# The first feed-forward of a decoder layer: from chunks of 352, 344 and 344 tokens to chunks of 128, 456 and 456

## The chip, the cores and the metric

The kernel runs on one core of a Trainium2 chip. A core has a matrix engine (TensorE, PE in the profile), a vector engine (VectorE, DVE), a scalar engine (ScalarE, ACT), a general engine (GpSimd, POOL), and a queue engine (SyncE, SP) that here issues most of the DMA transfers. Each engine works through its own instructions in order and waits on semaphores of the others. The metric is the device time of one execution, in microseconds (us); lower is better.

## The reference, cut to what matters

One layer over T = 16 + 1024 = 1040 tokens with D = 1024 and D_FF = 2816. The change lies in the first line of the sum:

```python
h = h + 0.5 * swiglu(rms_norm(h, ffn1_norm), ffn1_w_in, ffn1_w_out)      # "FFN1"
u = rms_norm(h, mix_norm) @ w_in
o = concat([hgrn2(...u...), stick_breaking(...u...)])
h = h + o @ w_out
h = h + 0.5 * swiglu(rms_norm(h, ffn2_norm), ffn2_w_in, ffn2_w_out)      # "FFN2"

def swiglu(h, w_in, w_out):
    g, u = split(h @ w_in, 2)              # w_in 1024 x 5632
    return (silu(g) * u) @ w_out           # w_out 2816 x 1024
```

All of it is in float32. The kernel splits each operand x of a product into a rounded part xh and a remainder xl = x - xh, and multiplies three times: wh xh, wl xh, wh xl.

## The kernel before, in words

Activations lie transposed: features on the 128 partitions, tokens along the free axis. A matmul loads a 128x128 block of weights (the stationary operand) and streams the tokens of a chunk past it. FFN1 cuts the 1040 tokens into THIRDS (line 29): 352, 344 and 344. Chunk 0 is computed plainly. Chunks 1 and 2 are the two columns of a 2x2 block matrix, multiplied by the seven-product (Strassen-Winograd) scheme: blocks B11, B21 (chunk 2), B22 and B12 (chunk 1), combinations T1 to T4 of them, and combinations of weight blocks made by POOL (`made`, L290 to L292). Seven products of each 2x2 block stand in for eight.

*Input product* (`fast_in`, L262). Weight columns come in pairs of 128; a `quad` (L339) computes such a pair for gate or up half: products B11, T2, B21, T3, T1, T4, B22 of twelve matmuls each, into PSUM banks qa, qb, qc, and beside them the four plain products of chunk 0 (`alone`, L325, bank qd), 84 + 48 matmuls a quad, 22 quads. Each weight block is split in `operand` (L275): wh on ACT (L277), wl on DVE (L279), three buffers; raw blocks of 256 KB come in through SP with eight buffers. The gate goes through Silu on ACT, the up half is multiplied on DVE (L418 to L428), and POOL makes the combinations T1 to T4 of the activations for the output product (`combined`, L434 to L450) and stores them to DRAM. The first three weight pairs ("openers") run their six plain quads ahead, while rows of chunks 2 and 1 are still loaded, normalised (`norm_rows`, L640), transposed on PE (`turned`, L623, tile xps), evicted and combined (`first_block` L669, `first_combined` L685: differences on DVE, halved by `halve` L218, ACT L222 and DVE L223). Between quads, `turn_x` (L711) transposes the residual rows and stores them as xD.

*Output product* (`fast_out`, L489). First `plain_round` (L544): chunk 0 over all 22 blocks of w_out, eight PSUM banks, 528 matmuls of 352 columns at L554; it is issued after a point inside the last quads (`issue_after(self.last_p1)`), so that its loads come during them. Then seven steps A12, A11, S1, S2, S4, S3, A22 (L569 on), each over q = 0 to 10, twelve matmuls a q (L588), 924 of 344 columns. A q's weights (`left`, L523) and activations (`right`, L509) are split by `halved` (L514: L516 ACT, L518 DVE, four buffers); the ring of raw blocks has five. `load_h` brings the residual hT (eight loads). The RMS norm of the next block (`norm_steps`, L1430) runs beside the steps, one chunk at a time, and ends in the early k and v projection (`project_early`, L1501).

The order on PE is that of the program text (`manual_schedule`). The order on DVE, ACT, POOL and SP is set by a list scheduler when the program is built, from the text's order, priorities and its own estimates; on the chip each engine then follows that list. A tile waits for what last used its buffer, and a new pool waits, tile by tile, for what used the same memory before.

## Time and profile before

| | us |
|---|---|
| runs, median (lowest to highest) | 2103.28 (2100.52 to 2104.81) |
| profiled execution, span | 2101.1 |
| PE busy | 2028.4 (97%) |
| DVE busy | 1392.3 (66%) |
| ACT busy | 901.4 (43%) |
| POOL busy | 647.1 (31%) |
| FFN1: first product / last input product / last output product ends at | 15.2 / 502.1 / 741.4 |

The profile gives each engine's busy time, windows of it, single instructions with their line and tiles (an instruction's `out<-in`), and a chain of waits followed back from the last instruction. "idle before <- releaser" is the time an engine stood still ahead of an instruction and what ended it. The kernel's times and the span are of different executions.

### The profile page before, as it was taken

Reading aid. Unit: us, or ns where it says so; the run is one execution under the profiler, and the core shown is the slowest. Engines: PE = TensorE matmul, PEld = TensorE weight load, DVE = VectorE, ACT = ScalarE, POOL = GpSimd, SP = SyncE. Lnnn points to the kernel's source line nnn. Section 1 sums busy time; section 2 is a strip of 40 time slices with the busy share of each in tenths; the row PEclk is TensorE's granted clock in tenths of the full one; section 3 lists DMA queues with packets and bytes.
Section 4 is the critical chain, followed back from the end, with each engine's and each line's share of the span. In section 5 each row is a group of like instructions: output and inputs, shape, how many; then the busy total and the mean of one; then the engine's idle time right before and its main releaser. Section 6 shows DMA issues by size and latency. Waiting matters only on the chain.

```text
span 2101.1 us, 32170 instructions
## 1 busy us (share of the span) xinstructions
PE 2028.4 (97%) x11520; PEld 1830.6 (87%) x11520; DVE 1392.3 (66%) x2140; ACT 901.4 (43%) x1860; POOL 647.1 (31%) x710
## 2 busy tenths in 40 slices
PE   7999999999999999999999998998999999999998
PEld 6999999999999999988897887886788888878887
DVE  6875544555489942258878776659776676677674
ACT  8543333333465634456666514235233233234443
POOL 2475545452000002243334200012554464430000
PEclk9999999999999999999999999999999999999999
DMA  7643333325867635435454162234533332358364
GB/s 198 190 146 121 110 111 104 98 80 197 254 207 223 220 116 166 156 108 138 119 142 131 51 242 87 81 118 135 162 103 100 111 105 91 107 193 267 111 200 136
DMA packets 272566, 301.12 MB, mean 143 GB/s; under 512 B 24694, under 2 KB 199158, under 8 KB 272406
## 3 DMA queue, kind: packets, MB, share of 16 engines
q1 hardware_dynamic: 254710, 248.62, 39.1%
q0 software_dynamic: 16656, 50.44, 6.5%
q8 instruction: 91, 1.49, 0.3%
q14 instruction: 69, 0.57, 0.1%
q10 hardware_dynamic: 1040, 0.00, 0.0%
HBM read 216.42 MB, written 82.57 MB: 142 GB/s over the span
## 4 chain that ended last, share of the span: by engine, by line
PE 83%; DVE 7%; ACT 2%; issue 1%; DMA 0%; POOL 0%; SPq 0%; DVEq 0%; ACTq 0%; POOLq 0%
PE o L588 16%; PE qb L320 13%; PE qc L320 9%; PE qa L320 8%; PE qd L320 6%; PE proj L163 5%; PE proj L164 5%; PE proj L165 5%; PE o L554 4%; PE flip L1070 2%; PE lvl L839 2%; PE wo L164 1%; PE wo L163 1%; PE wo L165 1%; DVE keep L1216 1%
## 5 line engine op out<-in xcount | busy, mean ns | idle before, releaser
L320 PE MATMUL qb<-T,wh 128*128 128x344 f32 (+1 forms) x1056 | 311.6, 358 | 9.7 <-DVE u L362 5.8
L279 DVE TENSOR_TENSOR wl<-s,wh 128x512 fp32r<-128x512 f32 x176 | 202.5, 1151 | 112.6 <-ACT wh L277 109.9
L588 PE MATMUL o<-tl,wh 128*128 128x344 f32 (+1 forms) x616 | 219.1, 357 | 5.1 <-DVE tl L518 5.1
L320 PEld LDWEIGHTS qb<-T,wh 128*128 128x128 f32 x1056 | 193.0, 189 | 35.3 <-ACT wh L277 7.5
L588 PE MATMUL o<-th,wl 128*128 128x344 f32 (+1 forms) x616 | 218.8, 357 | 2.5 <-DVE wl L518 2.5
L588 PE MATMUL o<-th,wh 128*128 128x344 f32 (+1 forms) x616 | 218.6, 357 | 0.0
L320 PE MATMUL qa<-B,wh 128*128 128x344 f32 (+1 forms) x704 | 209.3, 361 | 0.0
L277 ACT CAST wh<-s 128x512 fp32r<-128x512 f32 x176 | 109.4, 622 | 224.5 <-PE qb L320 154.6
L163 PE MATMUL proj<-xh,wh 128*128 128x344 f32 (+2 forms) x576 | 204.9, 356 | 0.0
L164 PE MATMUL proj<-xh,wl 128*128 128x344 f32 (+2 forms) x576 | 199.5, 346 | 1.1 <-DVE wl L150 1.1
L165 PE MATMUL proj<-xl,wh 128*128 128x344 f32 (+2 forms) x576 | 198.7, 345 | 0.0
L279 DVE TENSOR_TENSOR wl<-raw,wh 128x512 fp32r<-128x512 f32 x172 | 153.4, 896 | 68.1 <-ACT wh L277 61.9
L277 ACT CAST wh<-raw 128x512 fp32r<-128x512 f32 x172 | 105.8, 620 | 194.0 <-PE qc L320 96.0
L320 PE MATMUL qb<-T,wl 128*128 128x344 f32 (+1 forms) x528 | 188.3, 357 | 0.0
L320 PE MATMUL qd<-X,wh 128*128 128x352 f32 x704 | 180.5, 324 | 1.3 <-DVE X L665 1.3
L516 ACT CAST th<-act 128x512 fp32r<-128x512 f32 (+2 forms) x176 | 95.2, 542 | 182.3 <-PE o L588 126.6
L292 POOL TENSOR_TENSOR s<-raw 128x512 f32<-128x512 f32 x88 | 125.0, 1421 | 94.4 <-DVE wl L279 70.1
L518 DVE TENSOR_TENSOR tl<-act,th 128x512 fp32r<-128x512 f32 (+2 forms) x176 | 105.7, 604 | 68.6 <-ACT th L516 68.6
L320 PEld LDWEIGHTS qa<-B,wh 128*128 128x128 f32 x704 | 128.6, 189 | 16.1
L588 PEld LDWEIGHTS o<-tl,wh 128*128 128x128 f32 x616 | 116.6, 190 | 19.3 <-DVE tl L518 6.9
L1216 DVE TENSOR_TENSOR_SCAN keep<-keep 128x144 f32<-128x144 f32 (+6 forms) x112 | 128.5, 1150 | 6.5 <-ACT keep L1212 4.4
L588 PEld LDWEIGHTS o<-th,wl 128*128 128x128 f32 x616 | 116.4, 189 | 15.9 <-DVE wl L518 3.8
(329 smaller groups left out, 4886.7 us busy)
## 6 DMA issues: line engine op xcount, KB each, us to landing
raw<-in_ffn_w_in_dram SPq DMA_DIRECT2D x208, 256.0 KB, 3.1
raw<-in_ffn_w_out_dram SPq DMA_DIRECT2D x176, 256.0 KB, 3.9
raw<-in_w_in_dram SPq DMA_DIRECT2D x28, 512.0 KB, 4.3
ks<-kD SPq DMA_DIRECT2D x32, 260.0 KB, 5.2
ak<-in_ffn_w_out_dram SPq DMA_DIRECT2D x22, 256.0 KB, 4.2
v<-vD SPq DMA_DIRECT2D x8, 576.0 KB, 5.0
hT<-xD SPq DMA_DIRECT2D x8, 520.0 KB, 7.5
xD<-xts POOLq DMA_DIRECT2D x16, 256.0 KB, 2.9
```

The lines of the kernel that those rows point to most:

```text
L163: nc.tensor.matmul(ps, wh[:, s], xs, start=k == 0, stop=False)
L164: nc.tensor.matmul(ps, wl[:, s], xs, start=False, stop=False)
L165: nc.tensor.matmul(ps, wh[:, s], xl[:, k, c0 : c0 + n], start=False, stop=k == nk - 1)
L277: nc.scalar.copy(hi, src)
L279: nc.vector.tensor_sub(lo, src, hi.bitcast(F32))
L292: op(t, x, y)
L320: nc.tensor.matmul(ps, a[:, k, :], b[:, k0 + k, :], start=start and k == 0 and i == 0, stop=k == 3 and i == 2, skip_group_check=True,)
L516: nc.scalar.copy(hi, src)
L518: nc.vector.tensor_sub(lo, src, hi.bitcast(F32))
L554: nc.tensor.matmul(ps[m], y[:, s], z, start=f == 0 and e == 0, stop=f == D_FF // P - 1 and e == 2,)
L588: nc.tensor.matmul(banks[bank][m], y[:, m * P : (m + 1) * P], z, start=start and q == 0 and e == 0, stop=q == nq - 1 and e == 2, skip_grou ...
L1216: nc.vector.tensor_tensor_scan(out=kv, data0=kv, data1=kv, initial=1.0 if last else keep[:, end : end + 1], op0=ALU.mult, op1=ALU.bypass,)
```

## The change

FFN1 takes chunks of 128, 456 and 456 tokens (CHUNKS); chunks 1 and 2 go by the seven products as before, now 456 wide. The 128 tokens (the "corner") change places with the weights: their xh and xl are the stationary operand, and weights stream past them, 256 columns in the input product (24 matmuls a quad, `corner_of`, L368 of the new text) and 512 in the output product (`corner_step`, L628, 132 matmuls beside the steps A12 and A11). The result is tokens by features, so it is transposed back: two transposes a weight pair (L394), split (L396, L397) and stored as actC, and eight at the end of A11 (`corner_back`, 647). The plain quads and the plain round are gone.

With that go: two openers instead of three, in the way in which FFN2 opens (gate and up products with B11 and B21 first); weights loaded as 128x4x256 (512 KB, three buffers) and split whole (`split_of`, L268 ACT and L270 DVE, tiles rh, rl of 128x1024, three buffers) where the corner needs them, other splits with two buffers; row buffers six; the combinations made from the split operands, the first difference of each on POOL (`gsub`, L796, L804, L813) and corrections by the remainder on DVE (L797 to L799, L805, L814; `halve` is L224, L225); in the output product a ring of four and three buffers for split operands, sk in a pool of its own, loads of w_out also into sk, and the norms spread over S1, S2, S3 and A22; the early k and v projection in chunks of 292, 292, 456 (EARLY).

```diff
+CHUNKS = [(0, 128), (128, 456), (584, 456)]
+EARLY = [(0, 292), (292, 292), (584, 456)]
 THIRDS = [(0, 352), (352, 344), (696, 344)]
...
+    def split_of(self, src, tag, bufs):
+        nc, wp = self.nc, self.wq
+        m = src.shape[2]
+        hi = wp.tile([P, 4, m], F32R, tag=tag + "h", name=tag + "h", bufs=bufs)
+        nc.scalar.copy(hi, src)
+        lo = wp.tile([P, 4, m], F32R, tag=tag + "l", name=tag + "l", bufs=bufs)
+        nc.vector.tensor_sub(lo, src, hi.bitcast(F32))
+        return hi, lo
+
+    def combined_block(self, x, op, y):
+        t = self.wq.tile([P, 4, P], F32, tag="s", name="s", bufs=3)
+        op(t, x, y)
+        return t
+
...
+    def weights_beside(self, col, w_in, opened, corner):
...
+        def part(w, i):
+            return [x[:, :, P * i : P * i + P] for x in w]
+
+        def small(src):
+            return self.split_of(src, "w", self.w_bufs)
+
+        if opened:
+            r = [self.split_of(load(h), "r", 3) for h in range(2)]
+            corner(0, r[0])
+            corner(1, r[1])
+            yield part(r[0], 0)
+            yield part(r[1], 0)
+        r0, r1 = load(0), load(1)
+        (a11, a21), (a12, a22) = part([r0], 0) + part([r0], 1), part([r1], 0) + part([r1], 1)
+        if not opened:
+            w0 = self.split_of(r0, "r", 3)
+            yield part(w0, 0)
+            corner(0, w0)
+        s1 = made(a21, add, a22)
+        s2 = made(s1, sub, a11)
+        yield small(s2)
+        if not opened:
+            w1 = self.split_of(r1, "r", 3)
+            yield part(w1, 0)
+            corner(1, w1)
+        yield small(made(a11, sub, a21))
+        yield small(s1)
+        yield small(a22) if opened else part(w1, 1)
+        yield small(made(a12, sub, s2))
+    def corner_of(self, x, n):
...
+        def go(h, w):
+            (wh, wl), (xh, xl) = w, x
+            if h == 0:
+                state["ps"] = pin.tile([P, 2 * P], F32, tag="qd", name="qd", bufs=2)
+            for k in range(4):
+                kb = 4 * h + k
+                for i, (a, b) in enumerate(((xh, wh), (xl, wh), (xh, wl))):
+                    nc.tensor.matmul(
+                        state["ps"], a[:, kb, :], b[:, k, :], start=kb == 0 and i == 0,
+                        stop=kb == 7 and i == 2, skip_group_check=True,
+                    )
+            if h == 1:
+                state["take"](state["ps"])
+
+        return state, go
+
+    def corner_pair(self, f, actC, pool, later):
+
+        nc = self.nc
+        kept = {}
+
+        def gate(ps):
+            kept["g"] = pool.tile([P, 2, P], F32, tag="cg", name="cg", bufs=2)
+            nc.scalar.activation(kept["g"].rearrange("p i f -> p (i f)"), ps, AF.Silu)
+
+        def up(ps):
+            g = kept["g"].rearrange("p i f -> p (i f)")
+            nc.vector.tensor_mul(g, ps, g)
+            later.append(turn)
+
+        def turn():
+            ps = self.pin.tile([P, 2, P], F32, tag="qd", name="ct", bufs=2)
+            for i in range(2):
+                nc.tensor.transpose(ps[:, i, :], kept["g"][:, i, :], self.ident)
+            t = pool.tile([P, 2, 2, P], F32R, tag="ct", name="cts", bufs=1)
+            nc.scalar.copy(t[:, :, 0, :], ps)
+            nc.vector.tensor_sub(t[:, :, 1, :], ps, t[:, :, 0, :].bitcast(F32))
+            nc.gpsimd.dma_start(actC[f // 2], t.bitcast(F32))
+
+        return gate, up
...
-            for f in ahead:
-                gate, up = plain_pair(f)
-                plain_quad(f * P, gate)
+            cg, cu = self.corner_pair(f, corner[1], ev0, later) if corner else (None, None)
+            return [quad(f * P, gate, opened, cg), quad(D_FF + f * P, up, opened, cu)]
+
+        opened = [q for f in range(0, 2 * openers, 2) for q in pair(f, True)]
+        for i in range(0, 2 * openers, 2):
+            for _ in range(2):
+                next(opened[i])
+                next(opened[i + 1])
                 yield
-                plain_quad(D_FF + f * P, up)
-                yield
-            ev["p"] = open_ev()
-            for f in ahead:
-                for q in pair(f):
-                    drain(q)
-                    between()
...
+        sk = (sums_pool or op).tile([P, nq, 512], F32, name="sk")
...
-            with self.tc.issue_after(self.last_p1.ins):
-                plain_round()
+        def corner_step(step, q, w):
+
+
+            late = step == "A11"
+            if q == 0:
+                kept["ps"] = [pout.tile([P, 512], F32, tag="xy"[late] + str(2 + i), name="c")
+                              for i in range(2)]
+            if late:
+                other = raw(1, 0, q)
+            else:
+                other = sk[:, q, :]
+                nc.sync.dma_start(other, block(1, 1, q))
+            t = ring.tile([P, 2, P], F32R, tag="actc", name="actc", bufs=self.ring_bufs)
+            nc.sync.dma_start(t.bitcast(F32), corner[q][:, 0 if late else 1])
+            for i, (wh, wl) in enumerate((w, halved(other, "w", 512))):
+                for e, (x, y) in enumerate(((t[:, 0], wh), (t[:, 1], wh), (t[:, 0], wl))):
+                    nc.tensor.matmul(kept["ps"][i], x, y, start=q == 0 and e == 0,
+                                     stop=q == nq - 1 and e == 2)
+            if late:
+                sub(ak[:, q, :], ak[:, q, :], other)
...
+                beside = corner and a in ("A12", "A11")
+                if beside and q == nq - 1:
+                    corner_step(a, q, (wh, wl))
...
+    def first_block(self, ci, rows, ops, pool=None):
...
+        def at(o, j):
+            return [t[:, j, :].bitcast(F32) for t in ops[o]]
+
+        t1, t2 = ([t[:, c : c + n] for t in tiles] for c in (0, n))
         for j in range(4):
-            sub(b11[j], b12[j], b11[j])
-            t2.append(pool.tile([P, n], F32, name=f"t2{j}"))
-            sub(t2[j], b22[j], b11[j])
+            (h, l), (bh, bl) = at("B11", j), at("B22", j)
+            gsub(t1[j], b12[j], h)
+            sub(t1[j], t1[j], l)
+            sub(t2[j], bh, t1[j])
+            add(t2[j], t2[j], bl)
             self.halve(ops["T2"], t2[j], j)
             yield
...
+            gsub(b12[j], bh, b12[j])
+            add(b12[j], b12[j], bl)
             self.halve(ops["T3"], b12[j], j)
...
+            gsub(t2[j], h, t2[j])
+            add(t2[j], t2[j], l)
+            self.halve(ops["T4"], t2[j], j)
...
-                    self.t_bufs, self.in_bufs = 2, 8
+                    self.t_bufs, self.in_bufs, self.w_bufs = 2, 3, 2
...
+                    self.row_bufs = 6
+                    rows = [self.rows_of(0, rp, nc.sync), self.rows_of(2, rp, nc.sync)]
...
                     with tc.high_priority():
-                        self.first_plain(rows[0], junk, plain)
+                        self.first_plain(rows[0], junk, xc)
+                        self.norm_rows(2, rows[1], junk)
+                        self.first_block(2, rows[1], ops)
                     with tc.issue_after(self.root.ins):
                         next(steps)
+                    rows.append(self.rows_of(1, rp, nc.sync))
                     next(steps)
-                    rows.append(self.rows_of(2, rp, nc.sync))
-                    self.norm_rows(2, rows[1], junk)
-                    ba = self.first_block(2, rows[1], rp, "ba", ops)
-                    next(steps)
-                    rows.append(self.rows_of(1, rp, nc.sync))
                     self.norm_rows(1, rows[2], junk)
-                    bb = self.first_block(1, rows[2], rp, "bb", None)
-                    made = self.first_combined(ba, bb, ops, rp, nw)
-                    for _ in range(3):
-                        for _ in range(4):
-                            next(made)
+                    self.first_block(1, rows[2], ops, rp)
+                    made = self.first_combined(ops, rp, nw)
+                    for _ in range(2):
+                        next(made)
+                        next(made)
                         next(steps)
                     drain(made)
...
-                    self.ring_bufs = 5
+                    self.ring_bufs, self.part_bufs = 4, 3
...
+                        if step == "S1" and q > 1:
+                            if q == 2:
+                                norms[0] = norm_steps(0, banks_of("01"), v, 1)
+                            next(norms[0])
+                        elif step == "S2" and 2 <= q < 6:
+                            if q == 2:
+                                norms[2] = norm_steps(2, lambda: [(self.pn, "nps")] * 2, v, 1)
+                            next(norms[2])
+                        elif step == "S3":
+                            next(norms[0], None)
+                            if 2 <= q < 6:
+                                if q == 2:
+                                    norms[1] = norm_steps(1, banks_of("23"), v, 2)
+                                next(norms[1])
                         elif step == "A22":
```

The generated order at three places. First PE's beginning. The names: xps are transposed rows, qd a PSUM bank, X chunk 0's split tokens, rh a split weight. Before:

```order
L633 MATMUL xps<-ident,row 128x128 x16
L633 MATMUL xps<-ident,row 128x96 x8
L320 MATMUL qd<-X_201,wh 128x352
L320 MATMUL qd<-X_201,wl 128x352
L320 MATMUL qd<-X_202,wh 128x352
```

After:

```order
L722 MATMUL xps<-ident,row 128x128 x20
L722 MATMUL xps<-ident,row 128x72 x4
L722 MATMUL xps<-ident,row 128x128 x12
L722 MATMUL xps<-ident,row 128x72 x4
L368 MATMUL qd<-rh,X_190 128x256
```

Chunk 2's rows are now transposed ahead of the first product, not only chunk 0's.

Second, DVE where the first T2 product's weight is split (the row `wl<-s`, s being a combined weight block; L223 and L225 are remainders of combined tokens, L279 and L270 remainders of weights, L704 and L814 differences of tokens). Before:

```order
L704 TENSOR_TENSOR ba_532<-ba_532,t_696 128x344
L223 TENSOR_TENSOR B_208<-bb_672,B_207 128x344
L279 TENSOR_TENSOR wl<-raw,wh 128x512 x2
L223 TENSOR_TENSOR T_216<-ba_520,T_215 128x344
L223 TENSOR_TENSOR T_216<-ba_524,T_215 128x344
L223 TENSOR_TENSOR T_216<-ba_528,T_215 128x344
L279 TENSOR_TENSOR wl<-raw,wh 128x512
L223 TENSOR_TENSOR T_216<-ba_532,T_215 128x344
L223 TENSOR_TENSOR B_208<-bb_674,B_207 128x344
L279 TENSOR_TENSOR wl<-raw,wh 128x512
```

After:

```order
L497 TENSOR_TENSOR sg<-qa,sg 128x456
L225 TENSOR_TENSOR T_199<-t_562,T_198 128x456
L814 TENSOR_TENSOR t_559<-t_559,B_195 128x456
L814 TENSOR_TENSOR t_560<-t_560,B_195 128x456
L814 TENSOR_TENSOR t_561<-t_561,B_195 128x456
L225 TENSOR_TENSOR T_205<-t_559,T_204 128x456
L225 TENSOR_TENSOR T_205<-t_560,T_204 128x456
L225 TENSOR_TENSOR T_205<-t_561,T_204 128x456
L814 TENSOR_TENSOR t_562<-t_562,B_195 128x456
L270 TENSOR_TENSOR wl<-s,wh 128x512 x2
```

Weight remainders stood between the combinations; now the remainder for the first T2 product stands behind nearly all of them.

Third, SP between the two products (raw from w_in are weights of the input product, from w_out those of the output product; xrow are residual rows). Before:

```order
L610 DMA xrow<-in_x_dram 16x512
L284 DMA raw<-in_ffn_w_in_dram 128x4x128 x15
L506 DMA raw<-in_ffn_w_out_dram 128x512 x2
L511 DMA act<-act1p_102 128x352
L506 DMA raw<-in_ffn_w_out_dram 128x512 x2
L511 DMA act<-act1p_103 128x352
L511 DMA act<-act1p_104 128x352
```

After:

```order
L318 DMA raw<-in_ffn_w_in_dram 128x4x256 x8
L623 DMA sk<-in_ffn_w_out_dram 128x512 x4
L1532 DMA hT<-xD 128x1040 x4
L567 DMA raw<-in_ffn_w_out_dram 128x512
L572 DMA act<-act10B_98 128x456
L625 DMA actc<-actc_174 128x256
L567 DMA raw<-in_ffn_w_out_dram 128x512
```

The first four weight blocks for the corner (sk) and four of the eight loads of hT now stand ahead of the first block of the steps.

345 lines of the change are left out of this document (154 added, 191 removed).

## The prediction

> **What bounds the kernel now.** I read the page's busy shares first, then the chain of waits, then the windows. In the page, the shares and the chain by engine:
>
> ```profile
> PE 2028.4 (97%) x11520; PEld 1830.6 (87%) x11520; DVE 1392.3 (66%) x2140; ACT 901.4 (43%) x1860; POOL 647.1 (31%) x710
> PE 83%; DVE 7%; ACT 2%; issue 1%; DMA 0%; POOL 0%; SPq 0%; DVEq 0%; ACTq 0%; POOLq 0%
> ```
>
> TensorE (PE) is busy for 97% and is 83% of the chain, so fewer matmul columns should shorten the run wherever PE has work waiting. The windows ask where that holds in the part that changes (start to the end of the first feed-forward, FFN1; columns: length, then each engine's busy time):
>
> ```profile
> 0.00:78.20 78.20, 62.02 (x375) 58.89 (x376) 60.70 (x140) 61.73 (x120) 22.23 (x29) 0.98 0.63 167
> 78.20:502.40 424.20, 421.17 (x2678) 419.74 (x2677) 236.34 (x345) 148.90 (x275) 218.44 (x232) 1.00 0.38 119
> 502.40:741.40 239.00, 234.62 (x1476) 232.12 (x1475) 186.31 (x355) 128.37 (x261) 16.65 (x30) 0.99 0.73 230
> ```
>
> From 78.2 to 502.4 (the steady input product) PE has 3 us without work in 424; in the output product 4.4 of 239. Only the first 78 us are not PE's: it waits 16 us, while DVE is busy for 61 and ACT for 62. The chain passes from one product to the other, and ends FFN1, without a gap:
>
> ```profile
> 496.35 1.92 PE qd L320 x12
> 498.27 1.89 PE qc L320 x12
> 500.16 1.94 PE qd L320 x12
> 502.70 83.90 PE o L554 x525
> 735.77 5.69 PE o L588 x23
> ```
>
> So a saving of columns counts in full between 78 and 741 us, and the change can lose only where it makes PE wait: in the opening, or at 502 us.
>
> **The columns.** Twelve 352-wide matmuls take 1.92 us and twelve 344-wide 1.89 (rows above), which is 160 and 157.5 ns each. For other widths:
>
> ```profile
> 1487.48 2.72 PE qc L320 x12
> 1014.20 0.28 PE L1140 MATMUL oacc<-wu,v 128*128 128x256 f32 x1
> 1014.32 0.28 PE L1142 MATMUL oacc<-wu,v 128*64 128x256 f32 x1
> 31.46 1.34 PE L633 MATMUL xps<-ident,row 128*128 128x128 f32 x12
> ```
>
> 512 columns take 2.72/12 = 226.7 ns, 256 columns follow each other at 120 ns, a transpose takes 110. Between 344 and 512 that is 0.412 ns a column, so 456 columns take 157.5 + 112 x 0.412 = 203.6 ns. Input product, 22 quads: before 48 x 160 + 84 x 157.5 ns = 20.9 us each, after 84 x 203.6 + 24 x 120 ns = 20.0; 22 times that is 460.0 against 439.6, and 22 transposes of the corner add 2.4: **-18.0**. Output product: before 528 x 160 + 924 x 157.5 ns = 230.0, after 924 x 203.6 + 132 x 226.7 ns and 8 transposes = 218.9: **-11.1**. With PE never waiting, the change would bring 29 us.
>
> **The opening.** Before, PE starts on the plain quads at 15.17 us, after 24 transposes:
>
> ```profile
> 9.31 4.52 PE L633 MATMUL xps<-ident,row 128*128 128x128 f32 x24 [9.31 <-DVE ss_x L654]
> 15.17 0.43 PE L320 MATMUL qd<-X,wh 128*128 128x352 f32 x1 [1.34 <-DVE X L665]
> L665 DVE SCALAR_TENSOR_TENSOR X<-xps,g,X 128x352 fp32r<-128x352 f32 x8 | 4.0, 572 | 0.0
> L655 DVE TENSOR_SCALAR row<-row,ss_x 128x1024 f32<-128x1024 f32 x6 | 4.5, 749 | 0.1
> L646 DVE SCALAR_TENSOR_TENSOR junk<-row 128x1024 uint8<-128x1024 f32 x3 | 3.6, 1209 | 0.0
> 720.84 1.14 DVE wl L150
> L697 DVE TENSOR_TENSOR bb<-bb,bb 128x344 f32<-128x344 f32 x4 | 1.9, 508 | 0.0
> ```
>
> After, 40 transposes of chunks 0 and 2 stand ahead of the first product, and between the first row (about 7.9: two row scalings earlier than the 9.31 at which all three rows are ready) and the last evictions DVE's order has 8 corner evictions (at most 0.57 each), 4 row scalings (0.75), 2 squares (1.21), 3 weight remainders of 128x1024 (1.14, as at L150), 4 evictions of 456 (about 0.65) and small ones: 16.8 us, so PE starts at 24.7. Then come two corner products (2.9 each), four B products (2.4 each), 32 transposes of chunk 1 (3.5) and a wait of 3.6 for the fourth weight split, which has no fourth buffer: the transposes end at 48.7.
>
> From there T2's first product waits for the DVE order: 39 operations of 456 columns ahead of its weight's remainder. One of 344 takes 0.508 us, one of 512 0.68 (L518, below), so 0.62 each: 24.2 us, and 2.6 for a remainder, an eviction and a corner's pieces: 75.5. But twelve differences are now POOL's, interleaved with them. What the two do to each other shows at 65 to 75 us of the same opening:
>
> ```profile
> 65.89 5.44 POOL L292 TENSOR_TENSOR s<-raw 128x512 f32<-128x512 f32 x1 [4.95 <-DMA raw<-in_ffn_w_in_dram]
> 69.24 0.50 DVE L223 TENSOR_TENSOR T<-ba,T 128x344 fp32r<-128x344 f32 x1
> 70.09 1.78 DVE L279 TENSOR_TENSOR wl<-raw,wh 128x512 fp32r<-128x512 f32 x1
> 71.40 1.62 POOL L292 TENSOR_TENSOR s<-s,raw 128x512 f32<-128x512 f32 x1
> 71.80 3.13 DVE L223 TENSOR_TENSOR B<-bb,B 128x344 fp32r<-128x344 f32 x2
> ```
>
> A POOL operation of 1.27 us (L443, below) takes 5.44 while DVE runs on, and then DVE's 0.68 takes 1.78 and two of 0.5 take 3.13 under POOL: they take turns. Nine of POOL's twelve fall after 48.7; at 456/512 of 1.27 each holds DVE 1.15 us, 10.4 in all: T2 at **86**. Bounds: 75.5 if they run side by side, 90 if DVE also waits for a starved POOL. I take the turns, which the rows show.
>
> The Trainium skill's "SBUF — State Buffer" (Who interferes with whom) says that a DVE instruction with two SBUF inputs and a GpSimd instruction block each other for a whole instruction, whoever came first. The trace agrees (1.78 for 0.68, 5.44 for 1.27), and by that rule T2 comes at 86 and not 75.5; it speaks against this change.
>
> Before, T2 starts at 77.9 with six plain quads (46.1), the first B11 (1.9) and 72 transposes (7.9) done: 22.0 lost. After, 4 x (24 x 120 + 24 x 203.6 ns) = 31.1 and 8.2 of transposes are done by 86: 46.7 lost, **+24.7**. The second feed-forward (FFN2) opens in the manner that FFN1 takes over, and there PE waits where T3 reuses T2's bank after DVE's sum (waits of PE, 1440 to 1500 us: total, times, longest):
>
> ```profile
> PE qb L320 <- DVE u L362: 1.9, 2, 1.0
> ```
>
> Four such places at about 0.75 (456 columns for 512, and some overlap) add 3. A slow clock after the waits adds 2: the row ending the next fence shows a mean clock of 0.86 over 12 us around one wait. Input product: 502.4 - 18.0 + 24.7 + 5 = 514.1.
>
> The Trainium skill's "TensorE: Matmul & The Clock Gate" (Part 1, What's actually happening) has the array at half speed after about 3.4 us of idling, for as long again; by that three waits would cost 5 us, not 2, and the sum would be 3 higher.
>
> **The hand-over to the output product.** Before, the plain round's loads are issued during the last quads, and no wait shows. After, the first w_out load goes into memory that the last gate product (L501) frees, behind four loads of hT (2 MB), and the first remainder of an activation and the second w_out block wait for POOL's T4 combination (L516). FFN2 already hands over like this, though with its first weights loaded:
>
> ```profile
> 1871.73 0.39 PE L320 MATMUL qc<-B,wh 128*128 128x512 f32 x1
> 1872.76 0.68 DVE L518 TENSOR_TENSOR wl<-raw,wh 128x512 fp32r<-128x512 f32 x1
> 1873.36 0.68 DVE L428 TENSOR_TENSOR sg<-u,sg 128x512 f32<-128x512 f32 x1
> 1876.26 3.43 DVE L518 TENSOR_TENSOR tl<-act,th 128x512 fp32r<-128x512 f32 x1
> 1876.65 1.27 POOL L443 TENSOR_TENSOR t<-sg,t 128x512 f32<-128x512 f32 x1
> 1880.45 1.58 POOL L443 TENSOR_TENSOR t<-sg,t 128x512 f32<-128x512 f32 x1 [0.30 <-DMA act10T<-t]
> raw<-in_ffn_w_out_dram SPq DMA_DIRECT2D x176, 256.0 KB, 3.9
> hT<-xD SPq DMA_DIRECT2D x8, 520.0 KB, 7.5
> 1871.60:1884.00 12.40, 8.81 (x29) 5.95 (x28) 11.85 (x12) 1.66 (x3) 7.92 (x9) 0.86 0.84 268
> ```
>
> The last product of DVE ends 2.1 us after PE, and POOL's T4 ends (1882.03) 8.0 us after that (1874.04). So the second block's load is issued 10.1 us after PE's end, lands 3.9 later and needs a cast and a remainder: q = 1 starts 14.6 after, with 4.05 us of q = 0 done: **+10.5**. Lower bound: the first load alone, 2.1 + 3.9 + 0.6 = 6.6. Upper: 7.5 for a landing behind hT, 14. I take 10.5, since the waits are in the order.
>
> **The rest** of the output product: -11.1 from the columns, and +1.5 because the last norm before the early projection spreads 456 columns instead of 344. Behind it the engines' orders are nearly the old ones.
>
> **Sum**: +11.7 (514.1 against 502.4) + 10.5 - 11.1 + 1.5 = +12.6 on the profiled span of 2101.1: 2113.7. The runs' median, 2103.28, is 2.2 above that span: **2115.9, say 2115 us.**
>
> **Rivals.**
> Side by side (B): POOL does not hold DVE in the opening, T2 at 75.5, -10.5: about 2105. For it: at 69.24 DVE took its usual 0.50 while POOL was the one held. Against: 3.13 us for two of 0.5.
>
> The columns win (C, the other side): my walk of DVE's order is too slow and PE's own work sets the opening, so that T2 comes at 24.7 + 39.3 = 64: -22, 2093. It decides from T2 before 70 us (2115 - 16 = 2099). For it: DVE has 17 free us in the first 78. Against: the 39 operations stand ahead of the weight.
>
> Transfers (D): with the corner, each q of A12 and A11 moves 889 KB (two blocks of 262, 233 of activations, 131 of the corner's) in 12 x 203.6 + 6 x 226.7 ns = 3.8 us, 234 GB/s, plus hT. The old output product moves 230 GB/s at a mean DMA share of 0.73. If only 200 came through, each of 22 q's would take 4.44 us: +14, 2129. Against: 268 GB/s at 0.84, above.
>
> Not what it says (E): if the 528 corner products took 160 ns, as the plain ones do, and not 120, +21: 2136. Against: the two starts at 1014.
>
> **How the numbers follow.** Forecast 0.50; B 0.20; C 0.15; D 0.11; E 0.04. About 0.2% (4.2 us, 2099 to 2107.5) is what a measurement of this kernel tells from no change. B lies inside it, C below; forecast, D and E above: slower 0.64, same 0.20, faster 0.16. Range 2098 to 2128: the hand-over's 6.6 and B's 75.5 together give 2100, T2 at 90 and 14 us of hand-over 2122; D is taken in, most of C is not.
>
> **What would show it.** T2's first product near 86 us with DVE's L270 remainder as releaser, and DVE operations of 1.5 us and more at L797 to L814; below 76, B or C. PE idle for 6 to 11 us after its last input product (about 514 us), ended by DVE's L579; no idle there refutes the hand-over. FFN1's last matmul near 753 against 741.4. Wrong altogether if the quads take more than 20.1 us each.

## The result, and the profile after

The changed kernel takes 2132.71 us (median, 2132.54 to 2134.13), the kernel before beside it 2103.07 (2100.52 to 2104.81): a ratio of 1.0142, interval 1.0127 to 1.0156. It is slower, as forecast, but by 29.6 us and not by 12, and lies above the range. The profiled span is 2132.4 against 2101.1: +31.3, where the sum had +12.6. The span belongs to the longest of the four runs (2134.13); the medians differ by 1.7 us less.

The busy times on the page of the changed kernel:

```profile
PE 2020.1 (95%) x10626; PEld 1757.2 (82%) x10626; DVE 1385.4 (65%) x2040; ACT 869.9 (41%) x1741; POOL 655.4 (31%) x711
```

PE is busy for 8 us less (2028.4 before) in a run that is 31 us longer: some 40 us more of it are time without a matmul. The windows of the changed kernel show where that time lies (length, then busy time and instructions of PE, PEld, DVE, ACT, POOL; granted clock, DMA share, GB/s):

```profile
0.00:24.70 24.70, 9.03 (x36) 6.77 (x37) 17.97 (x45) 14.74 (x32) 3.65 (x10) 1.00 0.89 268
24.70:52.00 27.30, 23.25 (x137) 20.99 (x136) 14.50 (x38) 17.70 (x28) 6.75 (x14) 0.94 0.39 108
52.00:83.80 31.80, 18.80 (x99) 17.15 (x99) 29.75 (x34) 12.64 (x24) 20.30 (x16) 0.79 0.18 57
83.80:110.00 26.20, 19.20 (x83) 16.14 (x82) 15.42 (x25) 8.06 (x14) 9.16 (x8) 0.87 0.29 90
110.00:524.20 414.20, 408.36 (x2194) 373.71 (x2193) 221.14 (x282) 133.53 (x211) 207.08 (x216) 1.00 0.35 115
524.20:550.00 25.80, 14.17 (x56) 11.46 (x54) 9.06 (x14) 6.83 (x13) 7.20 (x9) 0.80 0.88 316
550.00:620.00 70.00, 70.00 (x327) 60.86 (x326) 47.65 (x74) 34.24 (x59) 0.00 (x0) 1.00 0.77 251
```

In the first 110 us PE is without work for 39.7 us (15.7, 4.1, 13.0 and 7.0 by these rows); between 52 and 84 DVE is busy for 29.75 of 31.8. At the hand-over another 11.6 us are missing. In the stretch with the most transfers beside the products, 550 to 620, PE is busy for 70.00 of 70. The last input product ends at 524.2 (before: 502.1), the last output product at 769.1 (741.4); the rest takes 1363.3 us (1359.6).

PE's instructions in the opening, out of the timeline (start, length, line, tiles; in brackets the idle time ahead and what ended it):

```profile
34.90 0.50 PE L368 MATMUL qd<-rh,X 128*128 128x256 f32 x2 [2.05 <-ACT rh L268]
50.59 1.46 PE L722 MATMUL xps<-ident,row 128*128 128x128 f32 x13 [0.21 <-ACT b L772]
69.48 0.79 PE L368 MATMUL qd<-rh,X 128*128 128x256 f32 x2 [10.61 <-ACT rh L268]
72.66 0.58 PE L368 MATMUL qd<-rl,X 128*128 128x256 f32 x1 [2.39 <-DVE rl L270]
89.72 0.75 PE L422 MATMUL qb<-T,wl 128*128 128x456 f32 x1 [5.46 <-DVE wl L270]
```

The transposes end at 52.05, and the T2 products, begun at 83.9, go on only at 89.72, when DVE's L270 has made the remainder. DVE in between:

```profile
52.20 4.63 DVE L797 TENSOR_TENSOR t<-t,B 128x456 f32<-128x456 f32 x3 [2.31 <-POOL t L796]
59.16 3.06 DVE L798 TENSOR_TENSOR t<-B,t 128x456 f32<-128x456 f32 x2
69.88 0.62 DVE L799 TENSOR_TENSOR t<-t,B 128x456 f32<-128x456 f32 x1
88.98 1.28 DVE L270 TENSOR_TENSOR wl<-s,wh 128x512 fp32r<-128x512 f32 x2
```

Up to 67 us, while POOL computes almost without a pause (51.0 to 66.5), an operation of L797 to L799 takes 1.5 to 1.7 us; one that starts while POOL stands still, as at 69.88, takes 0.62. The four evictions at 56.76 (L776), which read PSUM, keep their 0.62 each beside a busy POOL.

One steady quad in the chain of waits of the changed kernel has this group of twelve 456-wide products and this one of the corner:

```profile
301.62 2.48 PE qb L422 x12
306.56 1.44 PE qd L368 x12
```

That is 206.3 ns a wide product (the mean of many such groups; forecast 203.6) and 120 ns a corner product (forecast 120).

The hand-over, first by the chain of waits of the changed kernel, then by the timelines of SP, PE and ACT, and by windows of 5 us:

```profile
526.14 1.17 POOL t L516
527.59 5.44 DMA act110T<-t
533.10 1.15 POOL t L516
```

```profile
521.81 1.78 SPq L1532 DMA_DIRECT2D hT<-xD  x4
525.85 0.33 SPq L567 DMA_DIRECT2D raw<-in_ffn_w_out_dram  x1
526.23 1.09 SPq L572 DMA_DIRECT2D act<-act10B  x1
534.33 0.33 SPq L567 DMA_DIRECT2D raw<-in_ffn_w_out_dram  x1
```

```profile
534.48 1.89 PE L673 MATMUL o<-th,wh 128*128 128x456 f32 x4 [10.06 <-ACT th L577]
538.90 0.62 PE L628 MATMUL c<-wh,actc 128*128 128x512 f32 x2
545.78 0.47 PE L673 MATMUL o<-th,wh 128*128 128x456 f32 x1 [1.29 <-ACT wh L577]
```

```profile
532.82 0.62 ACT L577 CAST wh<-raw 128x512 fp32r<-128x512 f32 x1 [7.99 <-DMA raw<-in_ffn_w_out_dram]
```

```profile
525.00:530.00 5.00, 0.00 (x0) 0.00 (x0) 0.83 (x2) 0.00 (x0) 4.09 (x5) 0.83 0.96 354
530.00:535.00 5.00, 0.52 (x1) 0.50 (x2) 1.53 (x2) 1.61 (x3) 3.02 (x5) 0.50 0.78 307
535.00:540.00 5.00, 5.00 (x17) 4.30 (x16) 2.27 (x4) 1.19 (x2) 0.09 (x1) 0.65 0.74 228
```

After the last input product (524.2) the last gate product has freed memory for the first raw block at 525.85, right behind four loads of hT; it lands 7.0 us later, when ACT can start to cast it (532.82). The second raw block is issued at 534.33, as POOL ends the last of its combinations (533.10 + 1.15 = 534.25), which had waited for a store of 5.44 us. The first output product starts at 534.48; its first twelve take until 538.90, 4.4 us and not 2.5, at a granted clock of 0.50 and then 0.65.

### The profile page after: what moved, and what is told of

The parts are those of the page before. It is cut to its first block, busy times and chain, and to the rows that moved or that the text cites. A ratio compares the mean times of both kernels' runs of the same rounds, so it can differ in the third digit from the quotient of the medians.

```text
span 2132.4 us, 29699 instructions
## 1 busy us (share of the span) xinstructions
PE 2020.1 (95%) x10626; PEld 1757.2 (82%) x10626; DVE 1385.4 (65%) x2040; ACT 869.9 (41%) x1741; POOL 655.4 (31%) x711
## 4 chain that ended last, share of the span: by engine, by line
PE 84%; DVE 9%; ACT 2%; issue 2%; DMA 2%; POOL 0%; SPq 0%; DVEq 0%; ACTq 0%; POOLq 0%
PE o L673 17%; PE qb L422 16%; PE qc L422 10%; PE qa L422 10%; PE proj L165 5%; PE proj L166 5%; PE proj L167 5%; PE qd L368 3%; PE flip L1177 2%; PE lvl L946 2%; PE wo L166 1%; PE wo L165 1%; PE wo L167 1%; PE c L628 1%; DVE keep L1323 1%
## 5 line engine op out<-in xcount | busy, mean ns | idle before, releaser
L422 PE MATMUL qb<-T,wh 128*128 128x512 f32 (+1 forms) x912 | 296.5, 386 | 11.6 <-DVE u L457 6.0
L673 PE MATMUL o<-th,wh 128*128 128x456 f32 (+1 forms) x616 | 234.5, 382 | 11.4 <-ACT th L577 10.1
L673 PE MATMUL o<-tl,wh 128*128 128x456 f32 (+1 forms) x616 | 233.8, 381 | 4.1 <-DVE tl L579 4.0
L673 PE MATMUL o<-th,wl 128*128 128x456 f32 (+1 forms) x616 | 234.2, 382 | 2.8 <-DVE wl L579 2.8
L268 ACT CAST wh<-s 128x512 fp32r<-128x512 f32 x176 | 109.4, 622 | 312.2 <-PE qb L422 221.8
L270 DVE TENSOR_TENSOR wl<-s,wh 128x512 fp32r<-128x512 f32 x176 | 191.6, 1090 | 48.2 <-ACT wh L268 42.6
L422 PEld LDWEIGHTS qb<-T,wh 128*128 128x128 f32 x912 | 173.3, 190 | 45.0 <-ACT wh L268 9.4
L165 PE MATMUL proj<-xh,wh 128*128 128x344 f32 (+4 forms) x576 | 205.4, 357 | 1.6 <-ACT wh L150 1.6
L166 PE MATMUL proj<-xh,wl 128*128 128x344 f32 (+4 forms) x576 | 200.0, 347 | 0.8 <-DVE wl L152 0.8
L167 PE MATMUL proj<-xl,wh 128*128 128x344 f32 (+4 forms) x576 | 199.4, 346 | 0.0
L422 PE MATMUL qb<-T,wl 128*128 128x512 f32 (+1 forms) x456 | 176.0, 386 | 6.6 <-DVE wl L270 6.6
L577 ACT CAST th<-act 128x456 fp32r<-128x456 f32 (+1 forms) x154 | 92.0, 597 | 207.9 <-PE o L673 168.0
L673 PEld LDWEIGHTS o<-th,wh 128*128 128x128 f32 x616 | 116.4, 189 | 30.2 <-ACT th L577 10.3
L165 PEld LDWEIGHTS proj<-xh,wh 128*128 128x128 f32 x576 | 108.8, 189 | 10.0 <-ACT wh L150 1.9
L422 PE MATMUL qa<-B,wh 128*128 128x512 f32 x352 | 117.0, 396 | 0.0
```

The lines of the kernel that those rows point to most:

```text
L165: nc.tensor.matmul(ps, wh[:, s], xs, start=k == 0, stop=False)
L166: nc.tensor.matmul(ps, wl[:, s], xs, start=False, stop=False)
L167: nc.tensor.matmul(ps, wh[:, s], xl[:, k, c0 : c0 + n], start=False, stop=k == nk - 1)
L268: nc.scalar.copy(hi, src)
L270: nc.vector.tensor_sub(lo, src, hi.bitcast(F32))
L422: nc.tensor.matmul(ps, a[:, k, :], b[:, k, :], start=start and k == 0 and i == 0, stop=k == 3 and i == 2, skip_group_check=True,)
```

## The experiments

Each run had the kernel before beside it on the same chip (2103.07 to 2104.04 us). "Input end" and "output end" are the ends of FFN1's last input and last output product. The instructions of the opening and their order are the same in the change, e_ring_h, e_ring and e_hand, and T2 runs on between 87.7 and 90.3 in them: differences of up to 2.7 us in that column, and what follows from them at the input end, are the spread from one execution to the next.

| | median us | ratio to before (interval) | T2 runs on at | input end | output end | span |
|---|---|---|---|---|---|---|
| the change | 2132.71 | 1.0142 (1.0127–1.0156) | 89.7 | 524.2 | 769.1 | 2132.4 |
| m_width | (not the layer) | | | | | |
| e_nolo | 2124.89 | 1.0102 (1.0082–1.0122) | 80.4 | 512.7 | 760.7 | 2124.2 |
| e_dve | 2131.87 | 1.0139 (1.0112–1.0166) | 86.0 | 522.5 | 770.5 | 2133.0 |
| e_open | 2130.39 | 1.0128 (1.0110–1.0146) | 82.5 | 523.8 | 771.5 | 2131.2 |
| e_open3 | 2130.42 | 1.0126 (1.0109–1.0143) | 96.6 | 517.9 | 767.9 | 2131.6 |
| e_ring_h | 2127.94 | 1.0123 (1.0108–1.0138) | 87.7 | 522.3 | 760.7 | 2125.9 |
| e_ring | 2140.03 | 1.0171 (1.0154–1.0188) | 90.3 | 524.7 | 773.0 | 2139.4 |
| e_hand | 2131.27 | 1.0133 (1.0118–1.0148) | 87.8 | 522.2 | 764.2 | 2129.7 |
| e_both | 2123.68 | 1.0091 (1.0076–1.0106) | 96.1 | 517.2 | 754.6 | 2120.0 |

### What a column costs (m_width)

48 matmuls of each width, one behind the other into one PSUM bank, five widths also from another start column of the moving operand.

```python
WIDTHS = [(352, 0), (344, 0), (344, 8), (448, 0), (456, 0), (456, 8), (456, 4), (464, 0), ...]
for j in range(48):
    nc.tensor.matmul(t[:, :n], wr[:, P*(j%4) : P*(j%4)+P], xr[:, at : at + n], ...)
```

> Not the layer: 16 groups of 48 matmuls of float32r operands, one moving width each, the moving operand starting at column 0, 4 or 8 of its row, and nothing else. Theory (a width of 456 costs more than the line through 344 and 512 because the start or the end of the row is not on a 64-byte step, 16 columns): 448 and 464 columns lie on the line at 200 and 206.7 ns, 456 at start 0 takes what 464 takes (206.7), and starting at column 8 makes 512 and 464 dearer. Rival (the price is a straight line in the width, and 206.3 in the kernel comes from what runs beside it): 456 takes 203.3 ns at every start.

The run was made once. Its chain of waits (x96 and x144: two or three start columns):

```profile
15.99 14.90 PE p344a L47 x96
141.16 8.34 PE p384a L47 x48
30.88 9.92 PE p448a L47 x48
40.80 29.85 PE p456a L47 x144
101.22 22.11 PE p512a L47 x96
```

By the last 24 starts of each group, the first start column: 344 takes 153.3 ns, 384 173.3, 448 206.7, 456 and 464 208.9, 480 216.7, 512 226.7. A straight line from 344 to 512 would give 202.2 at 456. From 344 to 384 a column costs 0.50 ns, from 384 to 448 0.52, and from 448 to 512 0.31, so the widths in between lie above the line. The theory was right in that 456 takes what 464 takes, and wrong in its cause: 448, a multiple of 16 columns, should have lain on the line at 200 and took 206.7. The rival's straight line is refuted. Nothing ran beside these matmuls: 456 is dear by itself, and not by what goes on around it in the kernel. The start column counts too: from column 8, 512 takes 233.3 and 464 takes 211.1, dearer as the theory had it, and 456 takes 205.0 from column 4. The kernel's own prices are met only nearly (344: 157.5 there, 153.3 and 156.7 here; 456: 206.3 there, 205.0 to 208.9 here), and the reason for the bend stays open.

### What sets T2 (e_nolo, e_dve, e_open)

e_nolo leaves out 16 of DVE's operations in the opening (its combinations lack the remainders of the B blocks):

```diff
-            sub(t1[j], t1[j], l)
-            add(t2[j], t2[j], bl)
-            add(b12[j], b12[j], bl)
-            add(t2[j], t2[j], l)
```

> The changed kernel without the sixteen corrections of the combinations by the split operands' remainders in the opening (L797, L799, L805, L814); T1 to T4 of the tokens are then made from the rounded parts alone, so this leaves out a part of the computation. Theory (the opening is as long as DVE's whole list, wherever the first T2's weight stands in it): 16 operations of 0.62 us go, T2 runs from 78 to 80 us instead of 89.7 and T3 from 83 to 86 instead of 95.0, and the run takes 9 to 11 us less, 2122 to 2124. Rival (PE waits there for POOL, ACT or the weights' transfers): T3 not before 91, 2129 or more.

T2 starts at 80.2 and does not stop again; the next wait of the timeline is that of T3 for the bank:

```profile
83.61 0.47 PE L422 MATMUL qb<-T,wh 128*128 128x456 f32 x1 [0.72 <-DVE u L457]
```

The input product ends 11.5 us earlier. 16 x 0.62 = 9.9 are the operations left out, by their usual length. 3.1 us of it go again in the output product (248.0 us against 244.9), and the median gains 7.8 us, less than the 9 to 11 that were expected.

e_dve moves the twelve first differences from POOL to DVE:

```diff
-        gsub = nc.gpsimd.tensor_sub
+        gsub = nc.vector.tensor_sub
```

> The changed kernel with the twelve first differences of the opening on DVE again, not on POOL. Theory (DVE and POOL take turns): in the changed kernel DVE's operations between 50 and 80 us take some 10 us more than their usual times; twelve operations of 0.62 us (7.4 us) come to DVE, and the 10 go except where POOL's weight combinations still fall there, so T2's second matmul comes between 86 and 91 us instead of 89.7, and the run within 3 us of 2132.7. Rival (no turns, the long operations have another cause): T2 at 97 us and the run 7 us slower, 2140.

DVE has twelve operations more in its list, and yet T2 goes on 3.7 us earlier. PE's wait, and the first operations that took 1.5 us each in the changed kernel:

```profile
86.03 0.75 PE L422 MATMUL qb<-T,wl 128*128 128x456 f32 x1 [10.69 <-DVE wl L270]
```

```profile
52.58 1.17 DVE L797 TENSOR_TENSOR t<-t,B 128x456 f32<-128x456 f32 x2
```

Two take 1.17 us where POOL stands still. T2's time alone varies by 2.7 us, so the list itself is the better measure: from the first difference to DVE's last half of a T block it takes 36.9 us here (51.48 to 88.33), and 39.8 in the change (51.01 to 90.80); in e_ring_h, e_ring and e_hand it takes 39.5 to 39.7. So the work that was handed to POOL cost DVE about 3 us more than doing it. On the whole run that is within the measurement: 1.7 us are left at the input end, and none at the output end.

e_open puts the weight's remainder ahead of the combinations for T3, T1 and T4 in DVE's order, in the manner of the kernel before (both pairs of openers first):

```diff
...
         next(opened[0])
+        yield
         next(feed)
         made_yet.add("T2")
...
-                    for _ in range(2):
-                        next(made)
-                        next(made)
-                        next(steps)
+                    next(steps)
+                    next(steps)
+                    for _ in range(4):
+                        next(made)
+                    next(steps)
```

> The changed kernel, with the second pair's opening products ahead of the combinations in the text, and the weights of the first T2 and T3 products split behind the T2 combinations, before those of T3, T1 and T4. Theory (the first T2 waits for DVE's order, 39 operations ahead of its weight): T2 runs from about 74 us instead of 89.7, T3 from about 81, T1 (whose weight still stands behind T4's combinations) from about 90 instead of 97.6, and the whole gains 6 to 8 us, 2125 to 2127. Rival (PE was not held by the order but by DVE's total): T1 does not move, and the gain is under 2 us, 2131 to 2133.

T2 goes through at 82.3, but then T3 waits:

```profile
93.00 0.72 PE L422 MATMUL qb<-T,wh 128*128 128x456 f32 x1 [8.02 <-DVE u L457]
```

T1 starts at 97.5, in the changed kernel at 97.6, and the input end moves by 0.4. So the rival holds, though the median (2.3 us under the change) lies between the two expectations: not the place of the one remainder, but the whole of what DVE must do before the products flow, sets the opening.

### More cover for it (e_open3)

A third opener, so that PE has another 15 us of plain products while DVE combines:

```diff
-ops, nw, a["ffn1_w_in"][0], act1D, 2, ev0,
+ops, nw, a["ffn1_w_in"][0], act1D, 3, ev0,
...
-bufs=2 if (i, j) == (0, 0) else 1
+bufs=openers if (i, j) == (0, 0) else 1
...
-                    for _ in range(2):
-                        next(made)
-                        next(made)
-                        next(steps)
+                    for _ in range(4):
+                        next(made)
+                        next(steps)
```

> The changed kernel with three opening weight pairs instead of two (a third buffer for the first gate tile, six for the first products, and a uint8 scratch tile, to make room), combinations spread over four steps. It gives PE 15.5 us more work ahead of the first T2. Theory (the change lost cover: 31 us of products stand ahead of T2, before it was 48): DVE's list grows by 4 weight remainders of 1.2 us and two evictions, T2 runs near 96 us, but PE has 15.5 us more done by then, and the input product ends 7 to 10 us earlier: 2123 to 2126 us. Rival (the opening's length is set by something that grows with the openers, or the later quads are short of operands): gain under 3 us.

The input product ends 6.3 us earlier; the output product ends 1.1 earlier. Between the two, the waits of PE (total, times, longest) show:

```profile
PE o L673 <- ACT th L577: 15.8, 1, 15.8
```

In the change it was 10.1. The first output product starts at 533.9, nearly as in the change (534.5), though the input product ends 6.3 us earlier. That is not because something else comes at a fixed time: POOL's last combination comes 7 us earlier as well. The chain of waits of e_open3 shows what took its place:

```profile
527.37 3.26 DMA act110T<-t
530.64 2.50 DMA act<-act10B
```

Judging by what releases it, the first block now lies in other memory, since the third opener needs more buffers. Its activations are loaded only when the store of POOL's last combination has landed (527.37 + 3.26 = 530.63), while the change issued that load at 526.23, before POOL had made any of the last combinations. So 5.2 of the 6.3 us go again. The median gains 2.3 us: the number of the rival, but not its reason, since the cover itself works.

### The hand-over (e_ring_h, e_ring, e_hand, e_both)

e_ring_h takes the pools of the output product in another order, so that the ring of raw blocks gets memory that is free early, and loads the residual three q's later:

```diff
-                    self.ring = self.pool("ring1", ctx=c2, side="right")
-                    self.parts = self.pool("parts1", ctx=c2, side="right")
                     pn = self.pool("norm", ctx=c2, side="right")
                     ph = self.pool("h1", ctx=c2, side="right")
+                    self.ring = self.pool("ring1", ctx=c2, side="right")
+                    self.parts = self.pool("parts1", ctx=c2, side="right")
...
-                if a == "A12" and q == 3:
+                if a == "A12" and q == (6 if corner else 3):
```

> The changed kernel, with the output product's ring and split buffers placed in memory that the last weights of the input product free, instead of under the last gate products, and the loads of hT moved from q = 3 to q = 6 of step A12. Theory (the hand-over waits because its first loads reuse memory that the last gate product and POOL's T4 free late): the gap of 10.1 us after the last input product (524.4 us) falls below 2, the slow clock and the second gap behind it (3.5 us) go too, FFN1 ends 11 to 13 us earlier, 2120 to 2122 us. Rival (the loads are late because the transfers are slow or the DMA queues full there): the gap stays above 6, 2128 to 2132 us.

The first output product starts 1.7 us after the last input product, and the two products together end 8.4 us earlier. Of these, 2.0 stand already at the input end and are the spread of the opening; the output product itself is 6.4 us shorter (238.4 us against 244.9). The waits of PE from 500 to 800 us:

```profile
PE proj L165 <- ACT wh L150: 5.1, 1, 5.1
PE o L673 <- ACT th L577: 2.7, 1, 2.7
```

The 10 us are gone, but the early projection now waits for a weight of w_in for 5.1 us (1.6 in the changed kernel): of 8.4, the span keeps 6.5 and the median 4.8. The cause was right; the gain was smaller than expected (2127.94, not 2120 to 2122). What holds that weight stands in the chain:

```profile
782.63 0.27 DVE wm L1261
783.75 0.33 SPq L1264
785.09 4.53 DMA raw<-in_w_in_dram
```

Ahead of its load, SP's queue has stores of tiles that DVE clears (wm, L1261). In the change these go out at 772.87 and the load at 774.69; here DVE clears the tiles only behind the last norm. The wait is 5.1 to 5.6 us in all four forms with the pools in this order (at L165 and L166 together), also in e_ring, where FFN1 ends late; in e_nolo, where FFN1 ends at the same 760.7, it is 2.4.

e_ring is the first of the two edits alone.

> Of the two edits of e_ring_h only the order of the pools; the loads of the residual stay where the change has them, ahead of the first block's loads. Theory (the memory that the first load needs makes the 10 us, not the 2 MB of residual ahead of it): the wait ahead of the first output product falls from 10 us to under 3, last output product at 760 to 763, median 2127 to 2129, as e_ring_h. Rival (the residual loads count as much): the wait stays at 4 to 7 us, median 2130 to 2132.

It is slower than the change, by 7 us. Both expectations failed. The wait ahead of the first output product does fall (1.45 us), but one as long as before comes at another place. The chain of waits, then PE's timeline:

```profile
536.13 2.69 DMA act110T<-t
539.06 0.33 SPq L1532
543.16 10.10 DMA raw<-in_ffn_w_out_dram
```

```profile
526.32 1.10 PE L673 MATMUL o<-th,wh 128*128 128x456 f32 x4 [1.45 <-DVE sg L501]
554.51 0.75 PE L673 MATMUL o<-th,wh 128*128 128x456 f32 x1 [10.87 <-ACT th L577]
```

Now the residual hT (L1532) lies in the memory that POOL's last T4 frees: its first load is issued when the store of that tile is done (536.13 + 2.69 = 538.82), and the next raw block stands behind it in SP's queue and lands 10.1 us after its issue, behind the 4 MB of hT. Someone has to wait for that tile; what matters is who, and what stands behind it in the queue. By the output end e_ring loses 3.9 us to the change, and another 3.1 behind it, where the wait for w_in grows as in e_ring_h. The later loads without the new order of the pools were not run.

e_hand is e_ring_h with the eight loads of hT one a q from q = 2 on, in place of all at once.

```diff
-                if a == "A12" and q == 3:
+                if a == "A12" and q == 3 and not corner:
...
+                        if step == "A12" and 2 <= q < 10:
+                            nc.sync.dma_start(hT[:, q - 2, :], xD[q - 2])
```

> As e_ring_h, but the eight loads of hT go out one a q, at q = 2 to 9 of step A12, not all eight at q = 6. Theory (what is left of the hand-over's loss in e_ring_h, 2.7 us at 556 us, is activations queued behind 4 MB of hT): that wait goes, FFN1's output product takes 235.5 us from the last input product instead of 238.4, and the run 2124 to 2126 us. Rival (the DMA queues are full there whatever the order): the wait only moves, 2127 to 2129.

```profile
PE o L673 <- ACT th L577: 4.1, 1, 4.1
PE o L673 <- DVE tl L579: 3.2, 4, 1.2
```

The waits at L577 (2.7 in e_ring_h) and at DVE's tl (1.5) grow, and the output product ends 3.5 us later than in e_ring_h; the median is above both expectations. The first load of hT now stands at q = 2, waits there for the store of POOL's last combination, and is issued at 535.87; the block of q = 3, behind it in SP's queue, at 536.25, in e_ring_h at 525.28.

e_both has the edits of e_open3 and those of e_ring_h.

> Three openers as in e_open3, and the two edits of e_ring_h (buffers of the output product taken in another order, loads of the residual later). Theory (the gain of the third opener was eaten by the hand-over alone, so the two add up): last input product near 516 us (517.9 less the 2 that the later loads gave), no wait over 3 us at the hand-over, last output product 238 later, at 754; median 2118 to 2122, still slower than before. Rival (the second product's loads need those us anyway, so the wait only moves into its first blocks): last output product at 760 or later, median 2126 or more.

```profile
PE proj L165 <- ACT wh L150: 4.7, 1, 4.7
PE o L673 <- ACT th L577: 4.4, 2, 2.6
```

Input end 517.2, no wait over 2.6 us in the output product, output end 754.6 (forecast 754): the third opener's cover (7.0 us at the input end; 6.3 alone) and the shorter output product (7.6 us; 6.4 in e_ring_h) add up to 14.5. 2.1 us of that are not in the span (the wait of 4.7 for w_in), and the median is 9.0 under the change, 2 us above what was expected. It is the fastest of the changed forms, and still slower than the kernel before: 1.0091, interval 1.0076 to 1.0106. No form beats the kernel before.

## Why the prediction was right or wrong

The terms of the sum, against the two traces (the measured ones add up to the 31.3 us; the third and the sixth row are differences):

| term | forecast | measured | from |
|---|---|---|---|
| columns, input product | -18.0 | -13.7 | 22 quads of 20.20 us, 20.93 before, and transposes 2.4 |
| opening up to T2 | +24.7 | +28.4 | T2 at 89.7, not 86 |
| T3's stalls and the clock | +5 | +7.4 | input end +22.1, less the two above |
| columns, output product | -11.1 | -7.8 | 924 x 206.3 + 132 x 232 ns, and transposes 0.9 |
| hand-over | +10.5 | +13.6 | waits of 10.06, 1.29 and 0.28, and 1.9 at a low clock (4.4 for 2.5 us) |
| the last norm | +1.5 | -0.3 | output end +27.6, less input end, columns and hand-over |
| behind FFN1 | 0 | +3.7 | 1363.3 us, 1359.6 before |

**What bounds it: right.** From 110 to 524 us PE has gaps of 5.8 us, all before 143, and from 550 to the end of FFN1 4.0; the change loses in the opening and at the hand-over, and nowhere else by more than 4 us.

**The columns: mis-sized, 7.6 us of the 18.7 that were missed.** The step that failed is "between 344 and 512 that is 0.412 ns a column". The line was drawn between two widths of the trace, and at 456 the chip lies above it: 206.3 ns in the kernel, 205 to 209 alone. 2.7 ns more by 1848 wide products of the input product is 5 us. In the output product the 512-wide corner products took 232 ns, not 226.7.

**The opening: the mechanism right, its start 3.3 us late.** PE began at 25.3 (24.7), and the split it had no buffer for came at 34.90 (35.0). The step that failed is "the transposes end at 48.7": it was 52.05. The addends that the forecast names come to 47.3, so 1.4 of the 48.7 stood without a term. Behind 34.90 came what no term had: a wait for the second remainder of 0.85, four waits for ACT's evictions (L772) of 1.2 together, and products at half their pace (from 38.16 to 40.06 the wide ones start 0.38 us apart, not 0.206). A part is spread: in e_ring_h, e_ring and e_hand the transposes end at 50.3, 52.9 and 50.3. From there DVE's list took 37.7 us, forecast 37.3. That this fits so well is in part luck: DVE's operations follow each other after 0.55 us, not 0.62 (L225 at 82.94 and 83.48), which saves 2.7 us over 39 of them, and DVE stood still for 2.1 us in between. The operations slowed by POOL (all of them between 52 and 75 us, less the usual length of each) add up to 10.6, forecast 10.4, and e_dve shows the turns by taking POOL away. The Trainium skill's "SBUF — State Buffer" (Who interferes with whom), which the prediction set beside this term, agrees with both runs (1.5 to 1.7 us for an operation beside POOL, 0.62 without). Rival B (75.5) and C (under 70) are refuted. T2 at 89.7 lies at the upper bound of 90, but not for the reason of that bound, a wait for a starved POOL.

**The stalls behind T2: 7.4 for 5.** Behind T2, PE waited for the bank 3.3 us, for DVE's wl 2.5 and for ACT's wh 1.6: 7.4, of which 3.0 were there before (for the bank, at 114 and 143 us), so 4.4 came where 3 stood. The step that failed is "Four such places at about 0.75": the bank added only 0.3, and the splits of the weights, which had no term, added 4.1. What is left for the clock is 3.0, a difference and no row (T2's products start 0.38 us apart from 90.26 to 93.68, some 2 us more than usual): between the 2 taken from the trace before and the 5 that followed from the Trainium skill's "TensorE: Matmul & The Clock Gate" (Part 1, What's actually happening). The windows show a clock of 0.79 and 0.87 in the 58 us from 52 on.

**The hand-over: its place right, its length near the upper bound of 14.** The step that failed is "with 4.05 us of q = 0 done": the forecast took the second block's load as what ends the wait, and the first block as there in time. The second block came as forecast: its load is issued 10.1 us after PE's end (534.33). But the first block came late: its loads are issued at 525.85 and 526.23, 1.6 and 2.0 us after PE's end, and landed 7.0 us later, behind 2 MB of hT, at a DMA share of 0.96 from 525 to 530. PE stood still until 534.48, when ACT had cast the weights and then those activations, and q = 0 then ran in part at half pace. The lower bound (6.6) had the first load alone, at 3.9 us; the upper one, 14, put hT ahead of the second block and not of the first, so that 13.6 came near it for another reason. (By the 3.8 us that the prediction itself uses for a q under D, its term would be 10.8.) e_ring_h shows that the memory and the loads ahead make the wait: with both moved, 1.7 us are left. e_ring shows that the order of the pools alone does not do it; whether the later loads alone would, no run shows.

**The transfers (D) and the corner's price (E): refuted.** PE is busy for 70.00 of 70 us at 251 GB/s, and twelve corner products take 1.44 us. The prediction's own mark for "wrong altogether", quads over 20.1 us, was passed by 0.1, which is the price of the columns.

**Behind FFN1: left out.** The step "the engines' orders are nearly the old ones" stood at nothing, and 3.7 us came. Two waits of the early projection for a weight of w_in (1.6 at L165, 0.8 at L166) come to 2.4, 1.1 before, so they explain 1.3. The other 2.4 stay open; a part may be spread, since with the same two waits the rest takes 1359.6 in e_open and 1362.4 to 1363.7 in e_nolo, e_dve and e_open3.

**The chances.** Slower had 0.64 and was right; the range ended at 2128, because the upper bounds of the opening and the hand-over were both taken as rare, and the columns had no bound at all. (D's own 2129, which the range was said to take in, lies outside it.) Both terms came out near their upper ends (89.7 of 90, 13.6 of 14), which with the columns makes 14.4 of the 18.7 us; the stalls behind T2 (2.4) and the time behind FFN1 (3.7), less 1.8 at the last norm, make the rest.

## What to carry to other kernels

A price read off two widths is no price for a third between them: bound it from the next wider one (456 columns cost at most what 512 do, 226.7), and carry that bound into the range, since it is multiplied by thousands. What a change saves in one stage can be lost at the start of the next, because other buffers in the first put the next stage's tiles into other memory: in e_open3 5.2 of 6.3 us went that way, and with the hand-over mended both gains came (e_both). Read again who releases the first load after every such change. A tile that is freed late holds whoever is given its memory, and all that stands behind that one in its queue: change who waits and the queue together (e_ring against e_ring_h).

## What the runs showed of the hardware

The price of a float32 product (fp32r operands) is not a straight line in its columns: 344 at 153.3 ns, 384 at 173.3, 448 at 206.7, 480 at 216.7, 512 at 226.7; that is 0.50 to 0.52 ns a column from 344 to 448 and 0.31 from there on. The start column of the moving operand changes it by some per cent: 512 columns take 226.7 from column 0 and 233.3 from column 8, 456 take 208.9 and, from column 4, 205.0. Handing twelve of 51 small operations to POOL made DVE's list longer, not shorter: 39.5 to 39.8 us in four executions, 36.9 when DVE did all of them itself.
